# x on ScalarE's queue, two modulation steps as one block of rows, the rest in pairs

## The chip, the cores and the metric

The kernel runs on one core of a Trainium2 chip. The metric is the device time of one execution in microseconds (us), as the median of several runs; smaller is better. A profile of one execution goes with it, with the engines TensorE (PE, its weight loads PEld), VectorE (DVE), ScalarE (ACT), GpSimd (POOL) and SyncE (SP), and 16 DMA engines.

## The reference

One residual block of a decoder, in float32, on a sequence of 512 tokens with 1024 channels: a token mixer (a gated convolution with 31 taps beside latent attention with 8 heads) and an MLP of width 4096. What the change touches is the beginning and the first tap of the convolution:

```python
mod = silu(c) @ w_ada + b_ada            # c: (1, 1024), w_ada: (1024, 6 * 1024)
shift1, scale1, gate1, shift2, scale2, gate2 = split(mod, 6)
h = rms_norm(x, g_pre_mix) * (1.0 + scale1) + shift1
z = h @ w_in                             # GLU halves, q / kv latents, rotary key, gates
ua, ub = split(z[:, 0:2048], 2)
u = causal_depthwise_conv(ua * sigmoid(ub), conv_w, conv_b)    # 31 taps per channel
```

Everything behind it (layer norm, attention, the gated sum, the output projection, the MLP with squared ReLU, two post-norms with gates) is the same before and after.

## The kernel before, in words

The kernel keeps activations transposed: channels on the 128 partitions, 512 tokens along the free axis, so the 1024 channels are 8 steps k of 128. Nearly every product is made exact by three matmuls: each operand is split into a rounded part and a rest (ScalarE copies the rounded part, DVE subtracts to get the rest), and hi*hi, hi*lo and lo*hi are added in PSUM.

No instruction is issued where it is written. `emit` records the whole program with a `Planner` (class at line 179; `record`, 276; `plan`, 347). For each engine the planner simulates a clock with fixed costs (`cost`, 248, and for DMAs line 301 in `record`) and always takes the ready instruction with the smallest key: for TensorE its place in the program less `plan.boost`, for the others its due time less `plan.hurry`. SP is one engine of the five and issues most loads; stores that add come from POOL. The program is issued in the order that the plan gives, and each engine then runs its own instructions strictly in that order. Buffers come from two arenas and eight PSUM banks, whose places are chosen in up to 14 repeated passes; so a changed constant or instruction can move the order elsewhere too. In the profile nearly every instruction has the line of the planner's issue loop, 433; instructions are told apart by their tiles.

The beginning, which the change rewrites (lines 561 to 774):

- SP loads c, the four tiles of x (128 tokens by 1024 channels, 512 KB each), the rows of b_ada and g_pre_mix, and then for each step k the columns of w_ada for shift and scale (`ada_load`, 567; 128 columns of each, 1 MB) and 7 x 128 columns of w_in (`g1_load`, 583; 448 KB).
- silu(c) is made from a transposed c (`cT`). Each tile of x gets its sum of squares on ScalarE, the power -1/2 on POOL and its scaling on DVE; TensorE transposes it in 8 groups of four, ScalarE copies each group out of PSUM (`xv`).
- The modulation of step k is a sum over 1024 rows of w_ada, times silu(c). For steps 0 and 1 TensorE forms it as a row (`ada_sums` with `on_pe`: 8 matmuls with one column of `cT` as weights, 256 columns of w_ada streamed). For steps 2 to 7 DVE does it with 8 multiply-adds of 256 elements. Then `to_columns` (682) sums over partitions with a matmul against ones, or turns the row into columns, and DVE adds b_ada and forms (1 + scale) * g_pre_mix.
- `first_products` (695) makes h for the step (two ScalarE passes, one DVE subtraction), splits the weights and adds 7 x 3 = 21 matmuls of 512 tokens into seven PSUM banks. After eight steps these hold the first GLU columns.

Later, `conv_ops` (851) runs the convolution on DVE as 8 x 31 multiply-adds of 512 tokens, spread over the products that follow (`pump`); the first tap is a `tensor_scalar` with the bias in it.

Of the kernel before, what the change touches and what calls it, by code (L numbers as in the profile page):

```python
# [17 lines left out]
P = 128  # L18
# [26 lines left out]
PE0, CH0, PE1, CH1 = (0,1,2,3,4,5,6,7), 1, (0,1,2,3,4,5,6,7), 1  # L45
# [11 lines left out]
KGRP = ((1,), (2,), (3,), (4,), (5,), (6,), (7,))  # L57
HL, SQ = 5e3, False
EXCL = True
LAG, AJ = 3000.0, 1  # L60
# [118 lines left out]
class Planner:  # L179
# [96 lines left out]
    def record(self, eng, fn, a, k):  # L276
# [17 lines left out]
        o.lag = self.lag if fn == "dma_start" and eng == "sp" and outs[0].tensor.name.startswith("f_arena") else 0.0  # L294
# [52 lines left out]
    def plan(self):  # L347
# [15 lines left out]
        free["sp"] = 750.0  # L363
# [74 lines left out]
def tile_hybrid_block(  # L438
# [46 lines left out]
    nc.scalar.copy(onesr, ones)  # L485

    def emit(past, replay):
# [73 lines left out]
        plan.hurry = HX + 1e4  # L561
# [3 lines left out]
        plan.hurry = 0.0  # L565

        def ada_load(ks, step=KD // 2):
# [5 lines left out]
            for j in range(0, KD, step):  # L573
                if step == 1:
                    sp.dma_start(out=v[:, :, j], in_=src[:, 0:2, j, ks[0] * P:ks[0] * P + n])
                    continue
                for s in range(2):
                    sp.dma_start(out=v[:, s, j:j + step], in_=src[:, s, j:j + step, ks[0] * P:ks[0] * P + n])
# [18 lines left out]
        plan.hurry = 0.0  # L597
# [3 lines left out]
        def row_loads(i, *vecs):  # L601
            r = tile_of([56, P], F32, f"rows{i}")
            at = 0
            for nm, src in vecs:
                n = src.shape[1] // P
                sp.dma_start(out=r[at:at + n, :], in_=src[0].rearrange("(a p) -> a p", p=P))
# [4 lines left out]
        plan.hurry = HC - 1e3  # L611
        row_loads(0, ("bada", b_ada), ("gpm", g_pre_mix))
        plan.hurry = 0.0
# [11 lines left out]
        dve.tensor_scalar(cT, cT, 0.5, None, ALU.mult)  # L625

# [16 lines left out]
        pool.tensor_scalar(b1p[:, 0:8], col("bada", 8, 8), 1.0, None, ALU.add)  # L643
        pool.tensor_scalar(b1p[:, 8:16], col("bada", 32, 8), 1.0, None, ALU.add)
# [21 lines left out]
        fa.free(*xt)  # L666

# [14 lines left out]
        def to_columns(srcs, ks):  # L682
# [6 lines left out]
            ksl = slice(ks[0], ks[-1] + 1)  # L689
            dve.tensor_tensor(mod[:, 0, ksl], pb.v(bg)[:, ksl], col("bada", ks[0], len(ks)), ALU.add)  # L690
            for k in ks:
                dve.scalar_tensor_tensor(mod[:, 1, k:k + 1], pb.v(bg)[:, KD + k:KD + k + 1], b1p[:, k:k + 1], col("gpm", k),
                                         op0=ALU.add, op1=ALU.mult)

        def first_products(k, wb):
# [11 lines left out]
            for wi, hi in ((0, 0), (0, 1), (1, 0)):  # L707
# [7 lines left out]
        plan.hurry = HA - 1e3  # L715
        wbs = [g1_load(0)]
        ro = pb.v(bg)[0:1, 256:512].rearrange("p (s n) -> p s n", s=2)

        def ada_sums(ks, ada, on_pe=(), chains=1):
# [3 lines left out]
            srcs, bufs = [], []  # L723
            if on_pe:
                bufs.append(fa.alloc(2 * P))
                srcs.append((fa.v(bufs[0], "p (s n) -> p s n", s=2)[0:1], 1))
            sums = []
            at = 0
            for j in range(KD):
                aj = av[:, :, j]  # L730
                if j in on_pe:
                    pe.matmul(ro, lhsT=cT[:, j:j + 1], rhs=aj, start=j == on_pe[0], stop=j == on_pe[-1])
                    continue
                if len(sums) < chains:
                    bufs.append(fa.alloc(2 * n))
                    sums.append(fa.v(bufs[-1], "p (s n) -> p s n", s=2))
                    dve.tensor_scalar(sums[-1], aj, cT[:, j:j + 1], None, ALU.mult)
                else:
                    q = sums[at % chains]
                    dve.scalar_tensor_tensor(q, aj, cT[:, j:j + 1], q, op0=ALU.mult, op1=ALU.add)  # L740
                at += 1
            fa.free(ab)
            if on_pe:
                act.copy(srcs[0][0], ro)
            plan.boost = 1000
            to_columns(srcs + [(q, P) for q in sums], ks)
            fa.free(*bufs)
# [5 lines left out]
        ada_sums((0,), ada0, PE0, CH0)  # L753
        first_products(0, wbs[0])

        for ks in KGRP:
            plan.hurry = HA - 1e4 * ks[0]
            ada = ada_load(ks, 1 if ks[0] == 1 and PE1 else KD // 2)
# [5 lines left out]
            if ks[0] == 1:  # L764
                plan.hurry = H1
                ada_sums(ks, ada, PE1, CH1)
            else:
                ada_sums(ks, ada)
# [8 lines left out]
        row_loads(1, ("gpl", g_pre_mlp), ("cb", conv_b), ("cng", conv_norm_g), ("cnb", conv_norm_b),  # L777
# [1086 lines left out]
```

## Time and profile before

| | |
|---|---|
| median of 3 runs | 808.64 us (808.34 to 808.76) |
| profiled execution | 807.76 us |
| its span, first to last instruction | 805.6 us |
| granted TensorE clock | 0.998 |
| TensorE matmul busy | 98% of the span, 4450 matmuls |
| VectorE busy | 91%, 1052 instructions |
| ScalarE busy | 59%, 790 instructions |
| GpSimd busy | 7% |

In the views, "idle before" is the time for which an engine stood still ahead of an instruction, and "<-" what ended it. The page cuts the span into 40 slices of about 20 us, each with the busy share in tenths. A row of the timeline gives the start, the time from the first start to the last end of a merged group, the engine, the operation with output and inputs, and xcount. "SPq" rows are issues of DMAs, not the transfers. A matmul on four-byte data that is not rounded shows as two instructions. A busy time of TensorE includes waits inside a merged group, so its instruction counts are read along with it.

### The profile page before, as it was taken

Reading aid. Unit: us, or ns where it says so; the run is one execution under the profiler, and the core shown is the slowest. Engines: PE = TensorE matmul, PEld = TensorE weight load, DVE = VectorE, ACT = ScalarE, POOL = GpSimd, SP = SyncE. Lnnn points to the kernel's source line nnn. Section 1 sums busy time; section 2 is a strip of 40 time slices with the busy share of each in tenths; the row PEclk is TensorE's granted clock in tenths of the full one; section 3 lists DMA queues with packets and bytes.
Section 4 is the critical chain, followed back from the end, with each engine's and each line's share of the span. In section 5 each row is a group of like instructions: output and inputs, shape, how many; then the busy total and the mean of one; then the engine's idle time right before and its main releaser. Section 6 shows DMA issues by size and latency. Waiting matters only on the chain.

```text
span 805.6 us, 12015 instructions
## 1 busy us (share of the span) xinstructions
PE 789.3 (98%) x4450; PEld 687.6 (85%) x4450; DVE 735.8 (91%) x1052; ACT 476.6 (59%) x790; POOL 59.6 (7%) x121
## 2 busy tenths in 40 slices
PE   6999999999999999999999999999999999999996
PEld 3888988889897888878888889988998899889985
DVE  2899999999999999999898579899989978997998
ACT  5564463375886247238343268777667766777852
POOL 2001010000000000010000010001003300320023
PEclk9999999999999999999999999999999999999999
DMA  8999433010363272143997026149806940895176
GB/s 265 315 266 371 131 116 113 27 54 27 118 197 105 79 224 64 53 157 131 326 364 250 28 93 226 49 131 302 324 28 148 285 143 27 177 270 193 29 160 139
DMA packets 100364, 130.99 MB, mean 163 GB/s; under 512 B 8817, under 2 KB 67538, under 8 KB 100306
## 3 DMA queue, kind: packets, MB, share of 16 engines
q1 hardware_dynamic: 93970, 118.69, 44.7%
q0 software_dynamic: 6336, 11.54, 9.0%
q8 instruction: 35, 0.57, 0.3%
q14 instruction: 23, 0.19, 0.1%
HBM read 109.23 MB, written 20.97 MB: 162 GB/s over the span
## 4 chain that ended last, share of the span: by engine, by line
PE 84%; DVE 11%; issue 2%; ACT 2%; DMA 1%; POOL 0%; SPq 0%; DVEq 0%; ACTq 0%
PE psum L433 84%; DVE f_arena L433 6%; DVE r_arena L433 5%; ACT r_arena L433 1%; DMA rows<-in_b_ada_dram 1%; ACT f_arena L433 1%; DMA r_arena<-h_spill 0%; SPq L433 0%; POOL lns L433 0%; DVEq L1859 0%; POOL stats L433 0%; DVE lns L433 0%; DVE stats L433 0%; DVEq L433 0%; ACTq L433 0%
## 5 line engine op out<-in xcount | busy, mean ns | idle before, releaser
L433 PE MATMUL psum<-r_arena 128*128 128x512 f32 (+3 forms) x4108 | 749.4, 343 | 0.3 <-DVE r_arena L433 0.2
L433 PEld LDWEIGHTS psum<-r_arena 128*128 128x128 f32 x4108 | 647.8, 189 | 86.0 <-DVE r_arena L433 2.0
L433 ACT CAST r_arena<-f_arena 128x1024 fp32r<-128x1024 f32 (+4 forms) x249 | 236.6, 970 | 174.9 <-PE psum L433 115.2
L433 DVE TENSOR_TENSOR r_arena<-f_arena,r_arena 128x1024 fp32r<-128x1024 f32 (+5 forms) x259 | 278.0, 1101 | 26.5 <-ACT r_arena L433 23.7
L433 DVE SCALAR_TENSOR_TENSOR f_arena<-f_arena,cw 128x512 f32<-128x512 f32 x240 | 166.4, 754 | 0.0
L433 DVE TENSOR_TENSOR f_arena<-f_arena 128x1024 f32<-128x1024 f32 (+3 forms) x104 | 110.1, 1072 | 3.7 <-DMA f_arena<-in_w_mlp_in_dram 3.2
L433 ACT COPY f_arena<-psum 128x512 f32<-128x512 f32 (+4 forms) x107 | 57.5, 551 | 34.4 <-PE psum L433 30.4
L433 ACT ACTIVATE f_arena<-f_arena 128x512 f32<-128x512 f32 (+3 forms) x117 | 67.0, 593 | 17.2 <-DVE f_arena L433 16.2
L433 DVE SCALAR_TENSOR_TENSOR f_arena<-f_arena,cT 128x256 f32<-128x256 f32 (+1 forms) x70 | 54.4, 803 | 2.0 <-DMA f_arena<-in_w_ada_dram 1.6
L433 POOL DMA_DIRECT2D y_spill<-f_arena x40 | 34.8, 870 | 263.8 <-ACT f_arena L433 260.6
L433 DVE TENSOR_TENSOR f_arena<-psum,f_arena 128x512 f32<-128x512 f32 (+1 forms) x43 | 28.7, 677 | 12.1 <-PE psum L433 9.3
L433 PE MATMUL psum<-ident,f_arena 128*128 128x128 f32 x234 | 33.0, 280 | 5.2 <-DVE f_arena L433 5.2
L433 ACT ACTIVATE f_arena<-psum 128x512 f32<-128x512 f32 x35 | 20.5, 596 | 28.4 <-PE psum L433 21.2
L433 PEld LDWEIGHTS psum<-ident,f_arena 128*128 128x128 f32 x234 | 27.3, 143 | 11.0 <-DVE f_arena L433 5.5
L433 DVE TENSOR_TENSOR r_arena<-psum,r_arena 128x512 fp32r<-128x512 f32 (+2 forms) x57 | 36.0, 662 | 0.4
L433 ACT CAST r_arena<-psum 128x512 fp32r<-128x512 f32 (+2 forms) x57 | 30.0, 564 | 9.3 <-PE psum L433 8.9
L433 POOL TENSOR_TENSOR stats<-stats,nhalf 128x1 f32<-128x1 f32 (+1 forms) x17 | 12.3, 722 | 169.5 <-ACT stats L433 147.5
L433 ACT ACTIVATE r_arena<-f_arena 128x512 fp32r<-128x512 f32 (+3 forms) x21 | 13.5, 645 | 16.1 <-DVE f_arena L433 13.8
L433 ACT ACTIVATE r_arena<-psum 128x512 fp32r<-128x512 f32 x12 | 7.2, 598 | 24.5 <-PE psum L433 24.5
L433 POOL TENSOR_TENSOR lns<-lns,nhalf 128x4 f32<-128x4 f32 x1 | 2.0, 2046 | 251.4 <-DVE lns L433 251.4
L433 DVE CUSTOM_DVE_ANT_0 f_arena<-psum,mask 128x128 f32<-128x128 f32 (+3 forms) x32 | 15.0, 489 | 0.0
L433 DVE SCALAR_TENSOR_TENSOR f_arena<-f_arena 128x512 f32<-128x512 f32 (+1 forms) x18 | 13.3, 757 | 0.1
(94 smaller groups left out, 211.8 us busy)
## 6 DMA issues: line engine op xcount, KB each, us to landing
f_arena<-in_w_ada_dram SPq DMA_DIRECT2D x32, 512.0 KB, 5.0
f_arena<-in_w_mlp_in_dram SPq DMA_DIRECT2D x32, 512.0 KB, 9.4
f_arena<-in_w_mlp_out_dram SPq DMA_DIRECT2D x32, 512.0 KB, 5.7
f_arena<-in_w_in_dram SPq DMA_DIRECT2D x24, 512.0 KB, 4.4
y_spill<-f_arena POOLq DMA_DIRECT2D x40, 256.0 KB, 6.3
f_arena<-in_w_ada_dram SPq DMA_DIRECT2D x24, 256.0 KB, 5.9
f_arena<-in_x_dram SPq DMA_DIRECT2D x8, 512.0 KB, 7.4
h_spill<-r_arena SPq DMA_DIRECT2D x16, 256.0 KB, 6.6
```

The lines of the kernel that those rows point to most:

```text
L433: getattr(self.real[o.eng], o.fn)(*o.a, **o.k)
```

## The change

- The four tiles of x are loaded by ScalarE's queue instead of SP's. The constant copy `onesr`, ScalarE's first instruction, is now recorded in the plan, behind these issues.
- Steps 0 and 1 of the modulation are loaded as one block of 256 columns of shift and of scale (2 MB, eight loads of 256 KB), ahead of the rows of b_ada and g_pre_mix. A new function `ada_rows` adds it into one PSUM row bank with 16 matmuls of 256 columns, in the order in which the pieces come, and ScalarE copies out one row per step; `from_row` turns a row into columns.
- Steps 2 to 7 go in three pairs: one block of w_ada for two steps, and 8 multiply-adds of 512 elements per pair on DVE.
- Shift and scale of a step are formed by two ScalarE instructions instead of two of DVE; (1 + b_ada) * g_pre_mix is made ahead by one more POOL instruction.
- In steps 0 and 1 the order of the three products is hi*hi, lo*hi, hi*lo (weights first). Transposes of the first two groups of x come earlier in the plan's order (`XB`, `XK`).
- The first tap of the convolution is a ScalarE instruction with scale and bias.
- Planner constants: DMA cost per byte 0.043 instead of 0.040, corrections of landing times for the first loads (`XL`, -1460, 1500), due times of the first loads (`A0`, `R0`, `W0`, `XS`).

```diff
-PE0, CH0, PE1, CH1 = (0,1,2,3,4,5,6,7), 1, (0,1,2,3,4,5,6,7), 1
-KGRP = ((1,), (2,), (3,), (4,), (5,), (6,), (7,))
+KGRP = ((2, 3), (4, 5), (6, 7))
+A0, R0, W0 = -3e3, -1e3, -4e3
+XB, XK = 400, 2
+KLO = 2
+XS = (5e3, 4e3, 3e3, 2e3)
+XL = (0, -400.0, -800.0, -1200.0)
...
-            o.dma = b * (6.0 + 0.040 * n) / (16 * n) * (ADD if eng == "pool" else 1)
+            o.dma = b * (6.0 + 0.043 * n) / (16 * n) * (ADD if eng == "pool" else 1)
...
-        plan.hurry = HX
+        plan.hurry, plan.lag = HX + A0, 0.0
+        ada0 = ada_load((0, 1), 2)
         xt = []
         for t in range(NT):
+            plan.hurry, plan.lag = HX + XS[t], XL[t]
             b = fa.alloc(D)
-            sp.dma_start(out=fa.v(b), in_=x[t * P:(t + 1) * P, :])
+            act.dma_start(out=fa.v(b), in_=x[t * P:(t + 1) * P, :])
             xt.append(b)
-        plan.hurry = HA
-        ada0 = ada_load((0,), 1)
...
+        def ada_rows(ada):
+
+            ab, av = ada
+            rb = pb.alloc()
+            ro = pb.v(rb)[0:1].rearrange("p (s n) -> p s n", s=2)
+            rows_ = []
+            for h in range(4):
+                for s in range(2):
+                    for j in range(2 * h, 2 * h + 2):
+                        pe.matmul(ro[:, s], lhsT=cT[:, j:j + 1], rhs=av[:, s, j], start=j + s == 0,
+                                  stop=j + s == KD, skip_group_check=True)
+            fa.free(ab)
+            for i in range(2):
+                row = fa.alloc(2 * P)
+                act.copy(fa.v(row, "p (s n) -> p s n", s=2)[0:1], ro[:, :, i * P:(i + 1) * P])
+                rows_.append(row)
+            pb.free(rb)
+            return rows_
...
+            plan.boost = XB if k < XK else 0
...
-            ksl = slice(ks[0], ks[-1] + 1)
-            dve.tensor_tensor(mod[:, 0, ksl], pb.v(bg)[:, ksl], col("bada", ks[0], len(ks)), ALU.add)
             for k in ks:
-                dve.scalar_tensor_tensor(mod[:, 1, k:k + 1], pb.v(bg)[:, KD + k:KD + k + 1], b1p[:, k:k + 1], col("gpm", k),
-                                         op0=ALU.add, op1=ALU.mult)
+                act.activation(mod[:, 0, k:k + 1], pb.v(bg)[:, k:k + 1], AF.Identity, bias=col("bada", k))
+                act.activation(mod[:, 1, k:k + 1], pb.v(bg)[:, KD + k:KD + k + 1], AF.Identity, scale=col("gpm", k),
+                               bias=b1g[:, k:k + 1])
...
-            for wi, hi in ((0, 0), (0, 1), (1, 0)):
+            for wi, hi in ((0, 0), (1, 0), (0, 1)) if k < KLO else ((0, 0), (0, 1), (1, 0)):
...
-            ada = ada_load(ks, 1 if ks[0] == 1 and PE1 else KD // 2)
+            ada = ada_load(ks, 4 // len(ks))
...
-                            dve.tensor_scalar(fa.v(cacc[ct]), fa.v(upad[ct])[:, 0:T], cw[:, ct, 0:1], col("cb", ct),
-                                              ALU.mult, ALU.add)
+                            act.activation(fa.v(cacc[ct]), fa.v(upad[ct])[:, 0:T], AF.Identity, scale=cw[:, ct, 0:1],
+                                           bias=col("cb", ct))
```

More of the change, by code (lines that the diff above doesn't have):

```diff
@@ L293, in record @@
         o.cost, o.post = self.cost(eng, fn, outs, ins, k)
-        o.lag = self.lag if fn == "dma_start" and eng == "sp" and outs[0].tensor.name.startswith("f_arena") else 0.0
+        o.lag = self.lag if fn == "dma_start" and eng != "pool" and (outs[0].tensor.name.startswith("f_arena") or not self.ops[60:]) else 0.0
         o.post += self.slack if eng == "pool" else 0.0
@@ L484, in tile_hybrid_block @@
     onesr = const.tile([P, P], R32, name="onesr")
-    nc.scalar.copy(onesr, ones)
     def emit(past, replay):
@@ L558, in rstd @@
             pool.tensor_tensor(o, o, nhalf[:, :n], ALU.pow)
-        plan.hurry = HX + 1e4
+        plan.hurry = HC
+        act.copy(onesr, ones)
+        plan.hurry, plan.lag = HX + 1e4, -1460.0
         c8 = tile_of([8, P], F32, "c8")
         sp.dma_start(out=c8, in_=c[0].rearrange("(a p) -> a p", p=P))
-        plan.hurry = 0.0
+        plan.hurry = plan.lag = 0.0
         def ada_load(ks, step=KD // 2):
@@ L573, in ada_load @@
             for j in range(0, KD, step):
-                if step == 1:
-                    sp.dma_start(out=v[:, :, j], in_=src[:, 0:2, j, ks[0] * P:ks[0] * P + n])
-                    continue
                 for s in range(2):
@@ L605, in row_loads @@
                 n = src.shape[1] // P
-                sp.dma_start(out=r[at:at + n, :], in_=src[0].rearrange("(a p) -> a p", p=P))
+                q.dma_start(out=r[at:at + n, :], in_=src[0].rearrange("(a p) -> a p", p=P))
                 col0[nm] = (i, at)
@@ L609, in row_loads @@
             rows.append((r, at))
-        plan.hurry = HC - 1e3
-        row_loads(0, ("bada", b_ada), ("gpm", g_pre_mix))
-        plan.hurry = 0.0
+        plan.lag = 1500.0
+        plan.hurry = HX + R0
+        row_loads(0, sp, ("bada", b_ada), ("gpm", g_pre_mix))
+        plan.hurry = plan.lag = 0.0
         pos4 = tile_of([NT, P], I32, "pos4")
@@ L643, in emit @@
         pool.tensor_scalar(b1p[:, 0:8], col("bada", 8, 8), 1.0, None, ALU.add)
+        b1g = tile_of([P, 8], F32, "b1g")
+        pool.tensor_tensor(b1g, b1p[:, 0:8], col("gpm", 0, 8), ALU.mult)
         pool.tensor_scalar(b1p[:, 8:16], col("bada", 32, 8), 1.0, None, ALU.add)
@@ L666, in emit @@
         fa.free(*xt)
+        plan.boost = 0
         hT = [pair(T) for _ in range(KD)]
@@ L712, in first_products, with from_row, ada_sums @@
             w.free()
[L715 to L719, printed above, removed]
+        def from_row(row, ks):
+            plan.boost = 1000
+            to_columns([(fa.v(row, "p (s n) -> p s n", s=2)[0:1], 1)], ks)
+            fa.free(row)
+            plan.boost = 0
+            plan.hurry = 0.0
+        def ada_sums(ks, ada):
             n = len(ks) * P
             ab, av = ada
[L723 to L728, printed above, removed]
-            for j in range(KD):
[L730 to L737, printed above, removed]
-                else:
-                    q = sums[at % chains]
-                    dve.scalar_tensor_tensor(q, aj, cT[:, j:j + 1], q, op0=ALU.mult, op1=ALU.add)
-                at += 1
+            b = fa.alloc(2 * n)
+            q = fa.v(b, "p (s n) -> p s n", s=2)
+            for j in range(KD):
+                if j == 0:
+                    dve.tensor_scalar(q, av[:, :, j], cT[:, j:j + 1], None, ALU.mult)
+                else:
+                    dve.scalar_tensor_tensor(q, av[:, :, j], cT[:, j:j + 1], q, op0=ALU.mult, op1=ALU.add)
             fa.free(ab)
-            if on_pe:
-                act.copy(srcs[0][0], ro)
             plan.boost = 1000
-            to_columns(srcs + [(q, P) for q in sums], ks)
-            fa.free(*bufs)
+            to_columns([(q, P)], ks)
+            fa.free(b)
             plan.boost = 0
@@ L752, in emit @@
         plan.hurry = H0
-        ada_sums((0,), ada0, PE0, CH0)
-        first_products(0, wbs[0])
+        for k in range(2):
+            plan.hurry = HX + W0 - 5e3 * k
+            wb = g1_load(k)
+            plan.boost = BOOST0
+            plan.hurry = H0 if k == 0 else H1
+            from_row(row01[k], (k,))
+            first_products(k, wb)
         for ks in KGRP:
             plan.hurry = HA - 1e4 * ks[0]
-            ada = ada_load(ks, 1 if ks[0] == 1 and PE1 else KD // 2)
+            ada = ada_load(ks, 4 // len(ks))
             ada_end = len(plan.ops) - 1
```

16 lines of the change are left out of this document (7 added, 9 removed).

## The prediction

> **What bounds the kernel now.** I read the page first: TensorE's busy time and its slices.
>
> ```profile
> PE 789.3 (98%) x4450; PEld 687.6 (85%) x4450; DVE 735.8 (91%) x1052; ACT 476.6 (59%) x790; POOL 59.6 (7%) x121
> ...
> PE   6999999999999999999999999999999999999996
> ```
>
> TensorE is full in every slice but the first and the last. The change keeps the number and size of TensorE's matmuls, so it can only win or lose where TensorE waits. Next I cut the beginning into stretches; behind the busy times of PE, PEld, DVE, ACT and POOL stand the granted clock, the DMA share and GB/s.
>
> ```profile
> core 0 of [0], span 805.6 us
> core 0: us, PE busy (x) PEld busy (x) DVE busy (x) ACT busy (x) POOL busy (x), PEclk, DMA share, GB/s
> 2.50:10.00 7.50, 2.15 (x10) 1.56 (x9) 2.04 (x5) 4.89 (x11) 2.43 (x32) 1.00 0.98 346
> 10.00:15.00 5.00, 5.00 (x17) 1.72 (x17) 1.63 (x3) 0.90 (x3) 1.59 (x4) 1.00 0.86 247
> 15.00:20.00 5.00, 5.00 (x30) 2.69 (x28) 1.38 (x3) 4.29 (x8) 0.00 (x0) 1.00 0.94 274
> 20.00:25.00 5.00, 5.00 (x30) 3.50 (x28) 3.51 (x6) 3.49 (x7) 0.00 (x0) 1.00 1.07 323
> 25.00:50.00 25.00, 25.00 (x119) 20.66 (x120) 21.98 (x56) 12.13 (x15) 0.43 (x4) 1.00 1.13 312
> ```
>
> The DMA engines are near full from 2.5 us to 50 us, and the rate hangs on what is loaded: 346 GB/s while x comes in rows of 4 KB, 247 to 274 while w_ada comes in pieces of 128 columns (512 bytes), 312 for the later mixture. Between 10 and 15 us PE is called busy all the time, but with 17 instructions only. The timeline of TensorE shows what it did there.
>
> ```profile
> 10.60 5.07 PE L433 MATMUL psum<-f_arena,cT 128*1 128x256 f32 x16
> 15.60 0.88 PE L433 MATMUL psum<-ident,f_arena 128*128 128x128 f32 x6
> 16.41 0.60 PE L433 MATMUL psum<-ones,f_arena 1*128 1x1 f32 x4
> 16.94 0.76 PE L433 MATMUL psum<-ident,f_arena 128*128 128x128 f32 x5
> 17.63 3.61 PE L433 MATMUL psum<-f_arena,cT 128*1 128x256 f32 x16
> 21.18 1.53 PE L433 MATMUL psum<-ident,f_arena 128*128 128x128 f32 x12
> 22.46 1.17 PE L433 MATMUL psum<-r_arena 128*128 128x512 f32 x4
> ```
>
> The 16 instructions of the first row block take 5.07 us, the same 16 of the second 3.61: the first wait for w_ada piece by piece. From 15.60 on PE runs without a gap: second block, transposes of x, and at 22.46 the first product. So TensorE's idle time lies ahead of 15.6 us. The end of the first products:
>
> ```profile
> 56.62 8.24 PE L433 MATMUL psum<-r_arena 128*128 128x512 f32 x35
> 64.79 0.25 PE L433 MATMUL psum<-ident,rows 37*128 37x37 f32 x1
> ```
>
> From 22.46 to 64.79, that is 42.33 us, stand the 8 x 21 = 168 products with seven small sets of sums between them; 35 of them in 8.17 us give 0.233 us each, so 39.1 us of the 42.33 are products. This stretch is already nearly dense.
>
> Behind it, up to 360 us, a second engine is full too (the same columns as above, then TensorE's waits for DVE in 60 to 365 us):
>
> ```profile
> 50.00:360.00 310.00, 309.58 (x1640) 266.20 (x1638) 306.76 (x543) 165.30 (x334) 7.52 (x12) 1.00 0.39 125
> ```
> ```profile
> PEld psum L433 <- DVE r_arena L433: 1.4, 3, 0.6
> PEld psum L433 <- DVE f_arena L433: 1.1, 2, 0.8
> ```
>
> DVE has 306.76 of 310 us busy: a TensorE that comes earlier needs a DVE that comes earlier as well.
>
> **The change part by part.** *x by ScalarE's queue.* SP's queue now:
>
> ```profile
> 1.20 1.78 SPq L433 DMA_DIRECT2D f_arena<-in_x_dram  x4
> 3.02 0.72 SPq L433 DMA_DIRECT2D rows<-in_b_ada_dram  x1
> 3.78 0.36 SPq L433 DMA_DIRECT2D rows<-in_g_pre_mix_dram  x1
> 4.18 6.66 SPq L433 DMA_DIRECT2D f_arena<-in_w_ada_dram  x8
> ```
>
> x goes (1.78 us), and the two row loads move behind the first w_ada block, so w_ada issues from 1.2 instead of 4.18 us and x from about 0.7, side by side. The first block is twice as large (steps 0 and 1): 2.10 MB, in runs of 1 KB. With x's 2.10 MB that is 4.19 MB before the last row sum can end. For the zero of the clock I take x now (ScalarE's rows; the first is the square of the third tile, which waited for its load):
>
> ```profile
> 8.07 1.06 ACT L433 ACTIVATE r_arena<-f_arena 128x1024 fp32r<-128x1024 f32 x1 [0.39 <-DMA f_arena<-in_x_dram]
> ...
> 15.71 1.45 ACT L433 COPY f_arena<-psum 1x256 f32<-1x256 f32 x3 [4.78 <-PE psum L433]
> 17.04 0.95 ACT L433 CAST r_arena<-f_arena 128x896 fp32r<-128x896 f32 x1
> 17.88 0.82 ACT L433 ACTIVATE r_arena<-f_arena,mod 128x512 fp32r<-128x512 f32 x1
> ```
>
> Three tiles, 1.57 MB, had landed at 8.0; at 346 GB/s they took 4.5 us, so the zero is 3.5, with issue and completion in it. x issues 0.46 us earlier now: zero 3.2 (rounded up). 4.19 MB at 346 GB/s are 12.1 us: the last piece lands at 15.3.
>
> [...]
>
> *First two steps as one row block.* Same 32 instructions as in the two rows of 16, 2 x 3.61 = 7.2 us of PE, but all ahead of the first product. All but the last piece's two matmuls (four instructions, 0.9 us) run while pieces land: row sums end at 16.2. From there the path is today's from the end of the 5.07 us (15.67) to the end of the h pass (17.88 + 0.82 = 18.70), 3.03 us: copy, sums, shift and scale, h. First product at 16.2 + 3.0 = **19.2** instead of 22.46. Bounds: 18.4 (the load starts 0.8 earlier, since the queues start at 0.7) and, where x comes last, 20.0 (below).
>
> *What is left over then.* 32 transposes of x have to fit between x's landing and 19.2, with ScalarE's eight copies behind them (0.48 each by the row of three in 1.45). x alone would land at 3.2 + 2.10 / 0.346 = 9.3; sharing byte for byte with w_ada at 15.3. The planner's corrections for the four tiles (0 to -1.2 us against first come, first served, where about 2.9 MB are ahead of the last byte: 11.5) put it at 10.3, which I take as what this program is laid out for. From landing to scaled tile 2.9 us (8.07 to the end of this row, the same tile):
>
> ```profile
> 10.22 0.74 DVE L433 TENSOR_SCALAR f_arena<-f_arena,stats 128x1024 f32<-128x1024 f32 x1
> ```
>
> So copies can run from about 13.7 to 16.3, five, and one or two in ScalarE's pauses later. One or two of eight groups of four transposes remain after 19.2, 0.128 us each by the 1.53 us of twelve: I take 0.7 us (bounds 0 and 3.1).
>
> *Sum of the beginning.* 19.2 + 0.7 + 42.3 = 62.2 against 64.8: **-2.6 us**. Nothing in the 42.3 changes in number: the same products; in steps 0 and 1 only their order, which costs nothing.
>
> *Pairs.* Now both steps of a pair wait for 2.10 MB. Step 2's data is complete at 4.19 + 0.92 (two weights) + 2.10 = 7.21 MB; at 330 GB/s (between the rows of 312 and 346, runs of 1 KB lying between 512 bytes and 4 KB) it lands at 25.0. Behind it: two DVE sums (1.5), sums on PE (0.5), shift and scale (0.6), h (0.8), 3.4 us: 28.4. Steps 0 and 1 keep PE until 19.2 + 0.7 + 9.8 + 0.4 = 30.1. No stall; stalls begin under 7.21 / (30.1 - 3.4 - 3.2) = 307 GB/s.
>
> *DVE.* Rows by shape:
>
> ```profile
> L433 DVE SCALAR_TENSOR_TENSOR f_arena<-f_arena,cw 128x512 f32<-128x512 f32 x240 | 166.4, 754 | 0.0
> ...
> L433 DVE SCALAR_TENSOR_TENSOR f_arena<-f_arena,cT 128x256 f32<-128x256 f32 x42 | 18.7, 481 | 0.3
> ...
> L433 DVE TENSOR_SCALAR f_arena<-f_arena,cw,cols 128x512 f32<-128x512 f32 x8 | 4.4, 553 | 0.0
> ```
>
> A pair's sums take 8 instructions of about 0.75 instead of 16 of at most 0.48: 3 x 1.7 = up to 5 us less; eight first taps leave, 4.4 us. ScalarE takes eight taps at 0.82 (the h row has the same form), 6.6 us, hidden under its 165.30 of 310 us; cover gone, each costs 0.3 more than it does on DVE. Thus DVE gets 9 us lighter and lets TensorE keep the 2.6. Of TensorE's 2.5 us of waits for DVE I take 0.4 as saved (bounds 0 and 1.5).
>
> *At nothing.* Shift and scale on ScalarE: today 0.87 us from the end of the sums (17.01) to h; two instructions of at most 0.48 give 1.2, so +0.3 to -0.2. The row loads now land with w_ada at about 15.4, needed at 17; late, the first product waits by as much. Constant copy, extra POOL product and planner constants: no path.
>
> Total -2.6 - 0.4 = **-3.0 us**. The profiled execution took 807.76 (805.6 span and 2.2 around it), 0.9 under the median of the runs: 808.64 - 3.0 = **805.6 us**.
>
> **The rivals.** *All comes in full:* first product at 18.4, nothing left over, 1.5 us off DVE's waits: 18.4 + 42.3 = 60.7, -4.1 - 1.5: **803.0**. For it: x's early issue; against it: ScalarE's copies.
>
> *x lands last, no change.* If the two queues share byte for byte, x's last tile lands at 15.3, is scaled at 18.2, transposed, copied and passed to h (0.1 + 0.5 + 0.8, crossings 0.4) at 20.0, and 24 transposes (3.1) remain: 20.0 + 3.1 + 42.3 = 65.4, +0.6 - 0.4: **808.8**. In the trace of before two loads from two queues never meet in this stage, so nothing there excludes it. [...]
>
> *Pairs starve TensorE, slower.* If two queues with mixed run lengths only reach the 260 GB/s between the rows of 247 and 274, 7.21 MB land at 30.9, step 2 can start at 34.3 instead of 30.1: 4.2 us of stall; 10.22 and 13.24 MB, 10.3 us of products apart, give 1.3 each: 6.8 in all, head end 69.0, +4.2 - 0.4: **812.4**. It decides under some 282 GB/s, where the gain is used up. For it: those rows; against it: their 512-byte runs, which the change removes.
>
> **How the numbers follow.** Forecast 0.52, in full 0.20, x last 0.18, starving 0.10. A measurement here tells about 0.2% (1.6 us) from no change; a tenth of the forecast's case falls inside that. Faster 0.68, same 0.22, slower 0.10. The likeliest, 805.6, has its own range from 804.1 (first product at 18.4, nothing left over) to 807.2 (first product at 20.0, two groups more left over, 0.8 us); to hold 8 in 10 it reaches to the full gain and to x last: 803.0 to 808.9.
>
> **What would show it.** Timeline of after: x's last square at 10 to 11 us, row sums ending near 16.2, first product near 19.2, at most eight transposes behind it, the 37-row transpose or the last of the 168 products near 62; DMA rate of 3 to 25 us above 310; no wait of PE at the third step; DVE in 50 to 360 us with pauses. The forecast is wrong if x's squares wait until 15 us, if the products of step 2 wait for w_ada, or if the beginning is shorter and the end is not.

## The result, and the profile after

The changed kernel takes 814.43 us (median of 7 runs, 812.03 to 815.01), the kernel before 808.76 us on the same chip (7 runs, 808.23 to 810.58): ratio 1.0056, 95% interval 1.0039 to 1.0073. It is 0.6% slower, where 0.4% faster was forecast. Its runs lie in two groups, three from 812.0 to 812.4 and four from 814.4 to 815.0; the profiled execution is of the lower one, 812.03 us with a span of 810.3 us and a granted clock of 0.997, so the traces explain 4.7 us of span.

The page of the changed kernel, busy times and slices of TensorE:

```profile
PE 790.4 (98%) x4450; PEld 687.0 (85%) x4450; DVE 727.7 (90%) x1004; ACT 482.8 (60%) x816; POOL 61.1 (8%) x122
...
PE   5999999999999999999999999999999999999996
```

DVE has 8.1 us less to do (735.8 before), ScalarE 6.2 us more (476.6), TensorE as many instructions as before. Only the first slice differs: 5 instead of 6. The beginning of the changed kernel, in stretches with the columns of the prediction:

```profile
2.50:10.00 7.50, 1.11 (x3) 0.34 (x4) 0.51 (x3) 3.26 (x6) 0.94 (x29) 1.00 1.02 361
10.00:15.00 5.00, 3.58 (x11) 1.17 (x10) 2.62 (x4) 3.65 (x10) 2.95 (x4) 1.00 1.07 370
15.00:20.00 5.00, 5.00 (x26) 2.46 (x25) 0.39 (x1) 0.93 (x2) 0.00 (x0) 1.00 1.08 353
20.00:25.00 5.00, 5.00 (x30) 2.63 (x28) 1.39 (x3) 2.56 (x6) 1.08 (x2) 1.00 1.08 365
25.00:50.00 25.00, 23.98 (x115) 19.39 (x115) 21.60 (x31) 17.38 (x34) 1.05 (x7) 1.00 0.85 276
50.00:360.00 310.00, 308.95 (x1638) 265.73 (x1637) 302.11 (x523) 172.16 (x348) 5.77 (x10) 1.00 0.40 125
```

The loads got what they were meant to get: 353 to 370 GB/s up to 25 us, where it was 247 to 346 (in the 276 behind it stand 356 to 357 GB/s up to 40 us and 154 to 155 from there, where the loads of the beginning are through). But TensorE has 1.11 us of work before 10 us instead of 2.15, and a gap behind it. The timeline of the changed kernel shows who came late (rows of ScalarE's queue, ScalarE and TensorE):

```profile
0.74 5.96 ACTq L438 DMA_DIRECT2D f_arena<-in_x_dram  x4
...
6.72 1.28 ACT L438 ACT_TABLE_LOAD   x1 [6.72 <-DMA f_arena<-in_w_ada_dram]
8.02 0.30 ACT L438 CAST onesr<-ones 128x128 fp32r<-128x128 f32 x1
8.22 0.20 ACT L438 ACTIVATE tmp<-cT 128x8 f32<-128x8 f32 x1
8.33 1.04 ACT L438 ACTIVATE r_arena<-f_arena 128x1024 fp32r<-128x1024 f32 x1
...
8.89 1.86 PE L438 MATMUL psum<-f_arena,cT 128*1 128x256 f32 x4 [6.39 <-DVE cT L438]
...
12.17 1.12 PE L438 MATMUL psum<-ident,f_arena 128*128 128x128 f32 x4 [1.42 <-DVE f_arena L438]
...
12.50 1.06 ACT L438 ACTIVATE r_arena<-f_arena 128x1024 fp32r<-128x1024 f32 x1 [0.26 <-DMA f_arena<-in_x_dram]
...
19.07 4.05 PE L438 MATMUL psum<-f_arena,cT 128*1 128x256 f32 x18
...
27.11 3.27 PE L438 MATMUL psum<-r_arena 128*128 128x512 f32 x12 [0.59 <-ACT r_arena L438]
```

The four issues of x on ScalarE take 5.96 us; three of them are done at 2.1 us, the fourth is issued at 6.36 us. Behind it on the same engine stand the table load, the constant copy, the tanh of silu(c) and the squares of x, so TensorE waits 6.4 us for `cT`. The row sums end at 23.1 us, the first product starts at 27.11 us (22.46 before). The chain of waits in the first 30 us names the same path; columns are start, us, and what ran:

```profile
1.20 5.14 DMA f_arena<-in_w_ada_dram
...
6.36 0.34 ACTq L438
...
6.72 1.28 ACT L438
...
12.17 11.42 PE psum L438 x49
```

The fourth load of x waits for the landing of the first piece of w_ada: that lands at 6.34 us, and the issue goes out at 6.36. In the program as built the loads go x, c, w_ada, w_ada, x, w_ada, w_ada, x, w_ada, w_ada, x, so the fourth tile of x is the eleventh load and the piece it waits for the third, eight places before it. The other loads that a landing holds back in the first 15 us of this trace (issued at 4.14, 8.81, 11.51, 12.92 and 14.56 us) also go out 0.02 us behind the landing of the load eight places before them, and in the kernel before the two issued at 8.06 and 9.45 us do. The expectations below call such a place a slot. The planner counts eight loads in flight (`DEPTH`, in `plan`), but in its plan the fourth tile is the seventh load and waits for nothing.

Behind the first products, in the timeline of the changed kernel:

```profile
69.50 0.25 PE L438 MATMUL psum<-ident,rows 37*128 37x37 f32 x1
```

From the first product to the 37-row transpose ("the head" below, up to this row) it is 42.39 us (42.33 before), from there to the end of the span 740.8 us in both. So the 4.7 us lie ahead of the first product, all of them. The median is 5.7 us later; the 1 us more belongs to the upper group of runs, of which there is no trace.

### The profile page after: what moved, and what is told of

Read it like the earlier page. It is cut to its first block, busy times and chain, and to the rows that moved or that the text cites. A ratio compares the mean times of both kernels' runs of the same rounds, so it can differ in the third digit from the quotient of the medians.

```text
span 810.3 us, 11989 instructions
## 1 busy us (share of the span) xinstructions
PE 790.4 (98%) x4450; PEld 687.0 (85%) x4450; DVE 727.7 (90%) x1004; ACT 482.8 (60%) x816; POOL 61.1 (8%) x122
## 4 chain that ended last, share of the span: by engine, by line
PE 84%; DVE 9%; DMA 3%; issue 2%; ACT 1%; SPq 0%; DVEq 0%; POOL 0%; POOLq 0%; ACTq 0%
PE psum L438 84%; DVE f_arena L438 6%; DVE r_arena L438 3%; DMA f_arena<-in_w_ada_dram 2%; ACT r_arena L438 1%; DMA f_arena<-in_w_in_dram 0%; ACT f_arena L438 0%; SPq L438 0%; DMA rows<-in_q_norm_g_dram 0%; DVEq L1877 0%; ACT L438 0%; POOL stats L438 0%; POOLq L1877 0%; ACTq L438 0%; ACT onesr L438 0%
## 5 line engine op out<-in xcount | busy, mean ns | idle before, releaser
L438 DVE SCALAR_TENSOR_TENSOR f_arena<-f_arena,cT 128x1024 f32<-128x1024 f32 (+1 forms) x49 | 51.1, 1052 | 1.6 <-DMA f_arena<-in_w_ada_dram 1.1
L438 DVE TENSOR_TENSOR f_arena<-psum,f_arena 128x512 f32<-128x512 f32 (+1 forms) x43 | 28.6, 672 | 18.1 <-PE psum L438 15.4
L438 POOL TENSOR_TENSOR stats<-stats,nhalf 128x1 f32<-128x1 f32 (+1 forms) x17 | 14.7, 864 | 162.9 <-ACT stats L438 138.2
L438 ACT ACTIVATE f_arena<-f_arena,cols,cw 128x512 f32<-128x512 f32 x8 | 6.5, 814 | 18.0 <-DVE f_arena L438 11.5
L438 PE MATMUL psum<-f_arena,cT 128*1 128x256 f32 x32 | 9.4, 437 | 6.4 <-DVE cT L438 6.4
```

What stands on the lines that cost most here:

```text
L438: getattr(self.real[o.eng], o.fn)(*o.a, **o.k)
```

## The experiments

Four numbers tell a version: the issue of the fourth tile of x, the first product, the end of the head, and the rest of the span. Where no other kernel is named, the edit is to the changed kernel. The kernel before, run beside them, had 808.17 to 808.96 us; ratios are to it.

| | 4th x issue | first product | head end | rest | ratio (95% interval) |
|---|---|---|---|---|---|
| before | by SP | 22.46 | 64.79 | 740.8 | 1 |
| changed | 6.36 | 27.11 | 69.50 | 740.8 | 1.0056 (1.0039 to 1.0073) |
| e1 | 10.96 | 31.24 | 74.94 | 741.8 | 1.0105 (1.0088 to 1.0122) |
| e2 | by SP | 24.64 | 67.00 | 743.4 | 1.0039 (1.0026 to 1.0052) |
| e3 | 6.63 | 27.76 | 70.12 | 741.4 | 1.0059 (1.0045 to 1.0073) |
| e4 | 7.29 | 27.99 | 69.83 | 741.1 | 1.0060 (1.0045 to 1.0076) |
| e5 (of before) | by SP | 20.31 | 64.03 | 742.3 | 1.0026 (1.0015 to 1.0038) |
| e6 | 6.64 | 28.42 | 72.16 | 740.5 | 1.0060 (1.0045 to 1.0075) |
| e7 | by SP | 25.28 | 67.66 | 741.0 | 1.0026 (1.0017 to 1.0036) |
| e8 | by SP | 25.52 | 67.88 | 742.3 | 1.0043 (1.0031 to 1.0055) |
| e9 | 2.21 | 24.79 | 67.08 | 742.0 | 1.0037 (1.0023 to 1.0051) |
| e10 (of before) | by SP | 23.64 | 66.89 | 739.7 | 0.9999 (0.9990 to 1.0007) |
| e11 (of before) | by SP | 21.99 | 66.41 | 739.8 | 0.9996 (0.9987 to 1.0005) |
| e12 | 2.19 | 23.96 | 67.60 | 742.4 | 1.0030 (1.0020 to 1.0041) |

Two cautions for this table. Up to the first pair's loads at 17.3 us e10 has the instructions of the kernel before in the same order, and its first product came 1.2 us later in its one profile: TensorE began the first row block 0.7 us later, because the loads of b_ada and g_pre_mix landed later, and needed 0.5 us more for it, because it ran at half speed (below) until 15.3 us instead of 13.6 (worked out from the block's 5.58 us, at 427 and 216 ns between starts). So a difference of one us between two profiles decides nothing. And the rest moves by up to 2.6 us (e2) though its work is the same: a changed beginning gives another order and other waits later, in e2 1.28 us for DVE at the layer norm, ahead of 365 us.

### Is it the late silu(c), or the late fourth tile of x? (e1 to e4)

e1 records the fourth load of x behind the tanh, so that the tanh does not stand behind it:

```diff
-        for t in range(NT):
+        for t in range(NT - 1):
...
         act.activation(tmp8, cT, AF.Tanh, scale=0.5)
+        plan.after = len(plan.ops) - 1
+        act.dma_start(out=fa.v(xt[3]), in_=x[3 * P:, :])
```

> The changed kernel with one thing moved: ScalarE issues the fourth tile of x behind the tanh of c instead of ahead of it. Theory A (the fourth issue waits for a completion slot that the first w_ada piece holds until 6.3 us, and the table load and the tanh stand behind it on ScalarE, so the row sums start at 8.9 instead of about 4): cT is ready near 4.5 us, the row sums end at 16 to 18, the first product stands at 19 to 21 instead of 27.1, the time falls to 805 to 807.5 us. Theory B (the block of 2 MB and its 7.2 us of row matmuls ahead of the first product cost the time, whoever issues x): cT is early, but the first product stays at 25 to 27 and the time at 811 to 815 us.

Measured, timeline of e1:

```profile
0.74 1.39 ACTq L438 DMA_DIRECT2D f_arena<-in_x_dram  x3
2.17 1.28 ACT L438 ACT_TABLE_LOAD   x1 [2.17 <-issue]
3.75 0.21 ACT L438 ACTIVATE tmp<-cT 128x8 f32<-128x8 f32 x1
...
6.79 1.86 PE L438 MATMUL psum<-f_arena,cT 128*1 128x256 f32 x4 [3.28 <-DMA f_arena<-in_w_ada_dram]
...
10.96 0.33 ACTq L438 DMA_DIRECT2D f_arena<-in_x_dram  x1
15.82 1.06 ACT L438 ACTIVATE r_arena<-f_arena 128x1024 fp32r<-128x1024 f32 x1 [0.56 <-DMA f_arena<-in_x_dram]
```

The tanh runs at 3.75 us and the rows begin at 6.79 us, and yet the first product comes at 31.24 us: later in the program, the load is issued at 10.96 us only, and the first square behind it starts at 11.34 us, after 7.38 us in which ScalarE stood still for a landing of w_ada. The wait moved back on ScalarE became a longer one. Neither forecast covers this.

e2 gives the four loads of x to SP again (`act.dma_start` to `sp.dma_start`), the rest of the change stays.

> The changed kernel with x loaded by SP's queue again, all else as changed. Theory A: no issue stands on ScalarE, cT is ready near 3.5 us, x is in by 10 us, w_ada's block by 15 to 16; first product 19 to 21, time 805 to 808 us. Theory B: first product 25 to 27, 811 to 815 us. Theory C (a second queue is worth its issue time): slower than the run that only moves the tanh by 1 to 2 us.

Measured: first product at 24.64 us instead of 27.11. Of the 4.7 us the queue accounts for 2.5; 2.2 are left without it. At the end of the profiled execution nothing of it is left (span 810.4 us), since the rest is 2.6 us longer; over the runs the ratio is 1.0039 instead of 1.0056. Theory A's 19 to 21 us missed; theory B's 25 to 27 us are nearer, and its time came (811.90 us).

e3 leaves silu out (the modulation is made from c itself, so the result is another one), which takes tanh and two DVE instructions out of the path to `cT`.

```diff
-        act.activation(tmp8, cT, AF.Tanh, scale=0.5)
-        dve.scalar_tensor_tensor(cT, tmp8, 1.0, cT, op0=ALU.add, op1=ALU.mult)
```

> The changed kernel without the silu of c (the row sums use c / 2): tanh and its product are left out, the fourth issue of x still waits on ScalarE. If the late cT alone makes the loss: row sums from about 4 us, first product 19 to 21, time 805 to 807.5 us. If the fourth tile, which lands at 12.5 us, and the squares behind it also count: first product 22 to 25, time 808 to 812 us. Theory B: no change, 811 to 815 us.

Measured: the rows begin at 6.75 us, 2.1 us earlier, and the first product comes at 27.76 us, no earlier. `cT` alone was not what the first product waited for; the tiles of x, whose squares stand behind the same issue, were as late as in the changed kernel (the last square at 12.99 us). Of the three forecasts only theory B's, no change, came true.

e4 takes the pairs back (`KGRP = ((2,), (3,), (4,), (5,), (6,), (7,))`).

> The changed kernel with steps 2 to 7 one by one again (w_ada in 512-byte runs, DVE sums of 256 elements). Theory A: the beginning is as late as in the changed kernel, first product near 27, time 811 to 816 us. Theory D (pairs starve TensorE): the products run on without waits and the time falls to 807 to 810 us.

Measured: first product 27.99, head end 69.83 us, ratio as the change. Pairs cost nothing in the changed kernel.

### TensorE's slow first microseconds (e5 to e8)

In the kernel before, the two halves of a row instruction start 427 ns apart until 13.5 us, and transposes 213 ns; from then on 216 and 109, in the trace's records of single instructions. The same factor of two for two kinds of work at one moment is not a wait for pieces of w_ada. e5 is the kernel before with 24 transposes of the identity into a spare bank behind the transpose of c; e6 is the changed kernel with the same lines:

```diff
         pe.transpose(pb.v(bc)[:, 0:8], c8, ident[:8, :8])
+        wu = pb.alloc()
+        plan.after = len(plan.ops) - 1
+        for i in range(24):
+            pe.transpose(pb.v(wu)[:, (i % 4) * P:(i % 4 + 1) * P], ident, ident)
+        plan.after = None
+        pb.free(wu)
```

> The kernel before with 24 transposes of the identity more on TensorE between c's transpose and x's first (2.6 to about 7.7 us), whose result nobody reads. Theory E (TensorE works at half speed for about 6 us after it starts: row matmuls 427 ns apart, transposes 213, then 216 and 109; and from 7.8 us on it is full of work, so its speed sets the first product): rows run 216 ns apart from the first one on, the first product moves from 22.46 to 19.6 to 21 us, the time falls to 805.5 to 807.5 us. Theory F (the 427 ns are waits for w_ada's pieces, as the prediction had it): the rows stay at 427 ns, first product at 22.5, time 808.5 to 809.5 us.

Measured, timeline of TensorE in e5:

```profile
2.44 5.21 PE L433 MATMUL psum<-ident 128*128 128x128 f32 x24
...
9.88 3.62 PE L433 MATMUL psum<-f_arena,cT 128*1 128x256 f32 x16
...
15.45 3.64 PE L433 MATMUL psum<-f_arena,cT 128*1 128x256 f32 x16
...
20.31 0.94 PE L433 MATMUL psum<-r_arena 128*128 128x512 f32 x3
21.94 1.96 PE L433 MATMUL psum<-r_arena 128*128 128x512 f32 x6 [0.69 <-ACT f_arena L433]
```

The first row block takes 3.62 us instead of 5.07, as the second: it never waited for pieces. The first product is 2.15 us earlier; the products then wait for ScalarE's copies, which stand behind a rounding of w_in that had not landed, so the head ends only 0.8 us earlier, and the whole is not faster (809.92 us; theory E forecast 805.5 to 807.5).

> The changed kernel with the same 24 transposes of the identity. Theory E: the 8 row matmul halves and 11 transposes that ran at half speed between 8.9 and 16.3 us get faster, but some of it turns into waiting for x's late tiles; first product 24.5 to 26 instead of 27.1, time 810 to 812.5 us. Theory F: no change, first product 27, 812 to 815 us.

Measured: the first four row instructions run at full speed, then TensorE stands still for 2.26 us for x's tiles, and it is at half speed again until 18.7 us at least; first product 28.42 us, where theory E had 24.5 to 26. The granted clock, third from the end in a row of the stretches, shows this spell:

```profile
12.00:18.70 6.70, 6.25 (x22) 3.47 (x23) 2.66 (x4) 1.95 (x6) 2.01 (x3) 0.50 1.08 359
```

In e6 the speed won early was lost in the pause.

e7 gives only the fourth tile to SP (`(act if t < 3 else sp).dma_start`), e8 adds the 24 transposes to e7.

> The changed kernel with the fourth tile of x issued by SP, three by ScalarE: no issue on ScalarE waits for a completion slot. Slot theory (the fourth issue costs the changed kernel 2.5 us): first product 22.5 to 24.6, as with all of x on SP or somewhat earlier; time 808.5 to 811.5 us. Theory A in its first form (without the blocked issue the forecast comes true): first product 19 to 21, 805 to 807.5 us. Theory B (the block): no change against the changed kernel, 812 to 815 us.

Measured: first product 25.28 us, above the slot theory's 22.5 to 24.6; ratio 1.0026, the best of the changed versions.

> Both at once: fourth tile by SP and 24 transposes of the identity. Slot theory and theory E together: first product 20 to 22.5, time 806 to 809 us. If either is wrong: like the run with the other alone, 808.5 to 812 us.

Measured, timeline of TensorE in e8:

```profile
2.42 4.44 PE L438 MATMUL psum<-ident 128*128 128x128 f32 x24
10.11 1.54 PE L438 MATMUL psum<-ident,f_arena 128*128 128x128 f32 x6 [3.25 <-DVE f_arena L438]
```

Single starts are 213 ns apart up to 5.8 us, then 109; after the pause of 3.25 us they are 213 again. First product 25.52 us: no gain, as in e6, and the 20 to 22.5 us of the two theories together missed.

### Taking the wait away without moving anything; pairs alone (e9 to e11)

e9 has four loads of 512 KB instead of eight of 256 KB for the first block, so that four fewer loads stand ahead of x's fourth:

```diff
-        ada0 = ada_load((0, 1), 2)
+        ada0 = ada_load((0, 1), 4)
```

> The changed kernel with one number altered: the first w_ada block comes in four loads of 512 KB instead of eight of 256 KB. Nothing leaves a queue or an engine; only four fewer completion slots are taken ahead of x's fourth load, so this load finds a free one. Theory (ScalarE's issue of the fourth x tile waits for the slot of a w_ada piece, and everything behind it on ScalarE is late): the fourth issue goes from 6.36 us to 2.1 to 2.5 us, tanh runs before 4.5 us, cT is ready before 5.5 us instead of 8.83, TensorE starts its rows when the first 512 KB pieces are in (6 to 7.5 us) and the first product comes at 24.0 to 25.5 us instead of 27.11; head end 66.4 to 67.9, ratio to the kernel before 1.001 to 1.004. Rival (the wait is harmless, x and w_ada share the bandwidth and x's tiles come late anyway): the issue is earlier as well, but the first product stays at 26.8 to 27.5 us and the ratio at 1.0056.

Measured, timeline of e9 (ScalarE's queue, DVE, ScalarE and TensorE):

```profile
0.74 2.06 ACTq L438 DMA_DIRECT2D f_arena<-in_x_dram  x4
...
4.56 0.17 DVE L438 SCALAR_TENSOR_TENSOR cT<-tmp,cT 128x8 f32<-128x8 f32 x1 [0.96 <-ACT tmp L438]
...
7.93 0.46 ACT L438 ACTIVATE stats<-stats,epsc 128x1 f32<-128x1 f32 x2
8.88 1.58 DVE L438 TENSOR_SCALAR f_arena<-f_arena,stats 128x1024 f32<-128x1024 f32 x2 [3.95 <-POOL stats L438]
...
9.34 2.72 PE L438 MATMUL psum<-f_arena,cT 128*1 128x256 f32 x6 [5.94 <-DMA f_arena<-in_w_ada_dram]
```

The theory's numbers came: the fourth issue comes at 2.21 us, the first product at 24.79 us (forecast 24.0 to 25.5), 2.3 us of the 4.7 gone by one size. So the fourth load's wait for a landing is shown as a cause by taking it away in three ways (e2, e7, e9: 24.6 to 25.3 us) and by making it longer (e1). The other 2.2 to 2.8 us stay in all of them. The rows of e9 say how: x and w_ada now come in side by side (383 GB/s from 2.5 to 10 us), the first w_ada piece is in at 9.2 us, and the first tile of x, whose sum of squares was done at 5.9 us, is scaled only at 8.88, because in ScalarE's order its statistics stand behind the square of the second tile (done at 7.9). TensorE's first real work starts at 9.34 us instead of 7.80. From there to the first product it needs 15.45 us, before 14.66, for the same work (e12 takes this apart).

e10 is the kernel before with pairs for steps 2 to 7 alone (`KGRP = ((1,), (2, 3), (4, 5), (6, 7))`), e11 adds the 24 transposes to it.

> The kernel before with steps 2 to 7 in three pairs (KGRP alone); queues, order of x and the first two steps stay. Theory (the loss lies ahead of the first product, pairs neither starve TensorE nor gain anything by themselves): first product 22.3 to 22.6 us as before, head end 64.4 to 65.2, rest within 1.5 us of 740.84, ratio 0.998 to 1.002. Rival of the prediction (pairs starve TensorE, since both steps wait for 2.1 MB): a wait of 1 us or more at the first pair and a head end of 66 us or later, ratio 1.002 to 1.006. Third way (longer runs make the loads faster, and the products, which wait a little for data in the kernel before, close up): head end 63.5 or earlier, ratio 0.997 to 0.999.

Measured, timeline of TensorE in e10:

```profile
11.27 5.58 PE L433 MATMUL psum<-f_arena,cT 128*1 128x256 f32 x16
...
23.64 2.34 PE L433 MATMUL psum<-r_arena 128*128 128x512 f32 x9
...
35.84 7.66 PE L433 MATMUL psum<-r_arena 128*128 128x512 f32 x31 [0.70 <-ACT r_arena L433]
```

The ratio is 0.9999: pairs alone change nothing. The head end missed its forecast (66.89 instead of 64.4 to 65.2): 1.2 us of it lie in the first product (the two causes named above), 0.9 us behind it, 0.7 of them a pause of TensorE at the first pair, and the rest of the run is 1.1 us shorter. So a bit of the rival "pairs starve TensorE" is real in this order of loads, and paid back.

> The run before this one plus 24 transposes of the identity into a spare PSUM bank right behind the transpose of c (about 2.6 to 5 us of work whose result nobody reads, while TensorE would stand still). Theory (TensorE's first 6 us go at half speed, and in the kernel before alone the 2.15 us won by these transposes were lost again because the loads of 128 columns did not keep up): with pairs the loads do keep up; first product 20.2 to 20.5 us, head end 62.4 to 63.0, ratio 0.996 to 0.999. Rival (the loads are not what took the gain back; ScalarE and the tiles of x are): first product as early, head end 63.8 to 64.3 as without pairs, ratio 0.999 to 1.003.

Measured: first product 21.99 us, head end 66.41 us, ratio 0.9996. With pairs the loads do not keep up either: the last w_ada piece of step 1 is waited for at 20.18 us (0.44 us), ScalarE at 23.51 (0.58), the first pair as in e10. That theory missed.

### How much is half speed in the changed kernel? (e12)

e12 is e9 with 40 transposes of the identity (the diff of e6, with 40 for 24), enough to last until the first piece is in.

> The changed kernel with the first w_ada block in four loads of 512 KB (as e9, whose fourth x load did not wait) and 40 transposes of the identity into a spare PSUM bank behind the transpose of c, whose result nobody reads; the order of the instructions ahead of the first product is that of e9 otherwise. Theory (e9's six row instructions 427 ns apart between 9.34 and 11.98 us are TensorE's half-speed start, 6 x 0.21 = 1.3 us, and the rest of its 24.79 us is work in which TensorE hardly waits): the dummies run 213 ns apart for 3 to 4 us and then 109, they end near 9 us, the row instructions run 216 ns apart from the first; first product 23.4 to 23.9 us, still behind the 22.46 of the kernel before, head end 65.7 to 66.4; ratio 1.001 to 1.004, no better than the kernel before. Rival (the pieces of w_ada and the tiles of x land too late for a faster TensorE): rows 216 ns apart, but with waits for w_ada or x between them that take the 1.3 us back; first product 24.5 to 25.0 us. Second rival (the first rows are slow for another reason than TensorE's speed, for example the arriving pieces): rows stay 427 ns apart.

Measured, timeline of TensorE in e12, and behind it the row of the first products in e9:

```profile
3.55 6.29 PE L438 MATMUL psum<-ident 128*128 128x128 f32 x40
9.77 1.46 PE L438 MATMUL psum<-f_arena,cT 128*1 128x256 f32 x6
...
23.96 9.39 PE L438 MATMUL psum<-r_arena 128*128 128x512 f32 x33 [0.59 <-ACT r_arena L438]
```
```profile
24.79 8.04 PE L438 MATMUL psum<-r_arena 128*128 128x512 f32 x33 [0.58 <-ACT r_arena L438]
```

The six row instructions take 1.46 us instead of 2.72, 1.26 us as forecast; the second rival is out. The dummies ended at 9.8 us, 0.4 us after e9's start, so 0.83 us of it arrive at the first product. They are lost right behind it: the same 33 products take 9.39 us instead of 8.04, for eight of them start 427 ns apart instead of about 231. TensorE had fallen back to half speed for 3.41 us, as the granted clock shows:

```profile
20.74:24.15 3.41, 2.62 (x20) 2.11 (x19) 3.30 (x5) 3.10 (x8) 1.56 (x3) 1.00 1.08 368
24.15:27.56 3.41, 3.41 (x9) 2.63 (x9) 1.36 (x3) 3.41 (x8) 0.00 (x0) 0.50 1.09 356
27.56:31.00 3.44, 3.44 (x17) 2.81 (x16) 3.40 (x6) 2.42 (x4) 0.12 (x1) 1.00 1.10 355
```

So the head end, 67.60 us, missed its 65.7 to 66.4. No version of the change beats the kernel before.

e5 and e12 are both at full speed between TensorE's first real work and the first product, and so show what the order alone is worth: 12.3 us in the order of the kernel before (7.99 to 20.31), 14.2 us in that of the change (9.77 to 23.96), for the same matmuls. Behind the last row sum of e12 (20.2 us) stand copies, sums, shift and scale and h, 3.7 us, and TensorE has only 12 transposes and a few small sums to do meanwhile; in the kernel before the second row block lies over this path. e9's 2.3 us behind the kernel before are then a start 1.5 us later, 1.9 us by the order, and 1.1 us less by half speed (1.26 us of it instead of 2.34). Each figure is of one profile.

## Why the prediction was wrong, point by point

*"The first wait for w_ada piece by piece", PE's idle time lies ahead of 15.6 us.* This reading failed, and the gain hung on it. The 1.46 us between 5.07 and 3.61 were TensorE at half speed (e5). In the kernel before, TensorE had no pause from 9.7 us on, and little from 7.80. Ahead of its first product stand 32 transposes of x and 32 row instructions, at full speed 32 x 0.109 + 32 x 0.216 = 10.4 us, with the small sums, the changes between kinds and the half speed 14.66 us. The prediction saw that both row blocks stand there, but not that the change leaves all this work there, which faster loads can't shorten. e12, at full speed throughout this part, still needs 14.2 us from 9.77.

*Row sums end at 16.2, h 3.03 us behind them.* Of the 7.9 us between the forecast 19.2 and the measured 27.11 us, 6.9 lie in the row sums, which end at 23.1 us, and 1.0 in the path behind them: 4.0 us, and 3.7 in e2, e7, e9 and e12. The step that failed is that the row sums "run while pieces land" and end 0.9 us behind the last one. The pieces were even early: the last one landed at 14.54 us (forecast 15.3), with the load that waited for it on SP issued at 14.56, but 26 of the 32 row instructions came after that.

*x "from about 0.7, side by side"; first product 19.2, bounds 18.4 to 20.0.* It came at 27.11. Three issues went out as said, the fourth at 6.36 us. The queue was costed as if moved issues went out without waiting, though the eight w_ada issues on SP in the kernel before (6.66 us, in the prediction's own fence) showed issues being held back: the fifth of them goes out at 8.06 us, after a wait of 1.3 us for a tile of x. What stood behind them was counted on SP, where nothing computes, and not on ScalarE, where tanh and squares do. This is 2.3 of the 4.7 us (27.11 to 24.79 in e9).

*What would show it.* x's last square at 12.50 us (forecast 10 to 11), row sums ending at 23.1 (16.2), no transposes of x behind the first product (up to eight), head end 69.50 (62.2). The DMA rate was right, above 310 GB/s (353 to 370).

*"The row loads now land about 15.4", "at nothing".* No wait for them shows in the changed kernel. But the constant copy and the table load, off any path before, stand in the chain now, 1.6 us of ScalarE between the late issue and the tanh. The extra POOL product, put at no path, holds up the shift and scale of e9 by 0.30 us.

*Pairs, no stall.* Right in the changed kernel: TensorE starts the first pair without a wait for w_ada, and e4 without pairs is no faster. The rival's 260 GB/s did not occur. In the kernel before pairs cost a pause of 0.7 us (e10).

*x lands last, 808.8.* Its direction was right, its mechanism wrong: x's last tile came late by its issue, not by sharing byte for byte. In e9, where no issue of x waited, ScalarE takes up the last tile as it lands:

```profile
10.77 1.06 ACT L438 ACTIVATE r_arena<-f_arena 128x1024 fp32r<-128x1024 f32 x1 [0.25 <-DMA f_arena<-in_x_dram]
```

Sharing byte for byte would give 15.3. (Pieces of w_ada are twice as large in e9 as in the changed kernel.) The second queue won nothing here: the first product came at 24.64 us with all of x on SP (e2), and at 25.28 and 24.79 us with three or four tiles on ScalarE's queue and no wait there (e7, e9). In the changed kernel its issue cost time besides, 6.4 us of TensorE waiting.

*42.3 us unchanged.* Right: 42.39.

*DVE 9 us lighter, -0.4.* The load moved as worked out (8.1 us less on DVE, 6.2 more on ScalarE), and the rest of the span kept its 740.8 us. The waits of TensorE's weight loads in 60 to 365 us, of the changed kernel and then of the kernel before (us in total, times, longest; the rows for DVE of before stand in the prediction):

```profile
PEld psum L438 <- ACT f_arena L438: 2.6, 10, 0.6
PEld psum L438 <- ACT r_arena L438: 1.8, 6, 0.7
...
PEld psum L438 <- DVE f_arena L438: 0.8, 2, 0.6
PEld psum L438 <- DVE r_arena L438: 0.6, 2, 0.4
```
```profile
PEld psum L433 <- ACT f_arena L433: 2.5, 11, 0.3
...
PEld psum L433 <- ACT r_arena L433: 0.6, 3, 0.2
```

Waits for DVE are 1.4 us instead of 2.5, waits for ScalarE 4.4 instead of 3.1. So "hidden under ScalarE's 165.30 of 310 us" was too simple: ScalarE, busy for 172.16 of 310 us in the changed kernel, still held TensorE up for 1.3 us more. The taps alone were not run; that they are what ScalarE's waits grew by is argued, not shown. The forecast also let the whole keep all of an earlier head. In e2, e5, e8, e9 and e12, whose heads end earlier than in the kernel that they change, the rest is 1.2 to 2.6 us longer; in e10 and e11, whose heads end later, 1.0 to 1.1 us shorter. But e7's is 0.2 us longer only, and e1's 1.0 us longer behind a later head, so whether 2.6 us would have reached the end is not shown.

The forecast failed on the sign because both errors sit ahead of the first product: a gain of 3.3 us that TensorE's own work did not leave room for, and a wait of 2.3 us that was not seen. The chance of 0.10 for slower was held by the wrong mechanism alone.

Open: how the 2.3 us that stay when the wait is gone divide rests on single profiles (e12). Nor is it shown why the changed kernel's runs fall into two groups. A half-speed spell that comes in some executions and not in others, as below, would fit, but no profile caught it in this kernel. The mean granted clock of the runs points the same way: 0.997 to 0.998 in the three of the lower group, 0.994 to 0.996 in the four of the upper, and one spell of 3.41 us takes 0.002 off it; e4's runs split alike (two at 0.997, two at 0.994 and 1.2 to 1.6 us longer). The half speed at the end of the span, from 802.1 of 805.6 us in the profile of the kernel before and from 804.8 of 810.3 in that of the changed one, moves the mean as well, so this is a hint only.

## What to carry to other kernels

Before moving a DMA to an engine that computes, list what it must wait for (here the landing of the load eight places earlier in the program, at 6.34 us) and what stands behind it on that engine: on ScalarE the waiting issue held up the tanh, which ran at 8.22 us instead of 2.83. Before costing a gain from earlier data, add up the consuming engine's own work between its first start and the point that is to come earlier: if it is dense, only its start counts, and its order, which decides what covers the path behind it. And where one instruction takes twice as long in one place as in another, compare the start-to-start times of other kinds around it before calling it a wait; in the kernel before the clock column stood at 1.00 while TensorE was slow, up to 13.6 us.

## What the runs showed of the hardware

TensorE starts at half speed in every kernel here. In the kernel before and the changed one transposes are 213 ns apart, then 109, and halves of row instructions 427, then 216. In the other runs the first groups tell it: six row instructions take 2.72 us (e2, e7, e9), against 1.46 in e12 behind its dummies; four take 1.86 to 1.87 (e1, e3, e4), against 1.02 in e6; the first row block takes 5.58 (e10), against 3.62 in e11; and 24 dummies take 5.21 to 5.38 (e5, e6, e11) or 4.44 (e8) where 24 x 0.109 would be 2.6, e12's 40 take 6.29 where it would be 4.4. The clock column shows this first stretch as 1.00 (the rows up to 15 us of the kernel before), but later ones as 0.50 (e6 from 12.00 to 18.70 us, e12 from 24.15 to 27.56, in the rows above). With dense work the change came 3.3 to 3.6 us after the first transpose in e8 and e12, but 4.9 us in e5 and at least as late in e6 (from the rows of 24 and 40 dummies, at 213 and 109 ns each); with work broken by waits 5.8 us after in the kernel before (7.80 to 13.6) and 7.4 us after in the changed one (8.89 to 16.3). Behind a pause of 2.26 us (e6) or 3.25 us (e8) TensorE was at half speed again: in e6 for those 6.70 us at least, in e8 with six row instructions in 2.72 us at 13.14 us, while the 24 from 16.45 us on take 5.34.

Half speed also came behind shorter pauses. In the changed kernel, e1, e3, e6, e9 and e12 TensorE does only four tiny sums in the last 1.66 us ahead of the first product. In e12 the clock is at 0.50 for 3.41 us from 24.15 us on, 0.19 us behind the first product's start, and its first 33 products take 9.39 us, as e1's take 9.40, where e9's take 8.04. In e1, e6 and e12 the head takes 1.3 us longer (43.6 to 43.7 us from first product to its end instead of 42.3 to 42.4); in the other three the same pause costs nothing. What decides between them was not shown.
